# State-space branch: masked products, steps, one subtraction and the chunk recurrence as wide GpSimd calls, with fewer VectorE instructions

## The chip, the cores and the metric

The kernel runs on one core of a Trainium2 chip. That core has five engines that run side by side, each with its own in-order queue of instructions: TensorE (PE, with its weight loads shown apart as PEld), VectorE (DVE), ScalarE (ACT), GpSimd (POOL) and SyncE (SP, which here only starts transfers). They wait for one another through semaphores. The metric is the device time of one execution in microseconds (us), lower is better.

## The reference, cut to what matters

Two transformer-like blocks work on one sequence of 512 tokens of 1024 features. The first block has an attention branch and a state-space branch in parallel, then cross attention and a feed-forward part; the second has a gated delta rule, sparse attention and a mixture of experts. Only the state-space branch of the first block is touched. It has 32 heads in 8 groups of 4; the heads of a group share B and C. The sequence is cut into 4 chunks of 128 tokens, and every head runs in two directions, forward and backward. In plain notation, for one chunk and one head, with cs the running sum of the step sizes times a decay rate:

```
S   = B . C^T                                       (128 x 128, shared by the 4 heads)
E   = exp(min(cs_f[l] - cs_f[s], cs_b[l] - cs_b[s]))   forward and backward decay in one
M   = E * S * (dt_f[s] where l >= s, plus dt_b[s] where l <= s)
y   = M^T . x + dskip * x                            inside the chunk
h_f[c+1] = raw_f[c] + tot_f * h_f[c]                 states handed on, chunk by chunk
h_b[c-1] = raw_b[c] + tot_b * h_b[c]
y  += C . h_f * exp(cs_f) + C . h_b * exp(cs_b)      then gate, norm, projection
```

## The kernel before, in words

All matrix products of weights are done as three products of split operands (a high and a low part of each), so every weight that comes in is first split: ACT casts the high part (line 269), DVE subtracts to get the low part (line 272). Then PE runs the three products, `mm3`, lines 277 to 279, in tiles named `mm`.

The branch goes group by group. `ssd_in` projects B, C, x and z of a group and runs a short convolution over them (four DVE instructions per tile, line 638). `ssd_p1` does the part inside the chunks: transposes of x and B (`xt`, `bt`), the products B.C^T (`cb` on PE, copied by ACT to the tile `CB`), and then for each of the four chunks: weighted inputs `xw` (POOL), step tiles `D` (POOL: two masked products and their sum), the chunk's states `st` (PE, copied by ACT into `pv`), the two tiles `cs` that a DMA broadcasts from DRAM, their difference and minimum, the exponential, the products with `CB` and `D`, a skip term `sk` (POOL), and the products `yd` (PE). `ssd_p2` hands the states on from chunk to chunk, multiplies them with C (`yo`), gates the result and sums its squares; `ssd_p3` normalizes and transposes (`yt`).

The difference and the minimum are done head by head before the change, two instructions for each head:

```
for h in range(4):
    nc.scalar.activation(cb[0][:, h, :], cb[0][:, h, :], AF.Identity, bias=...)
    nc.vector.scalar_tensor_tensor(cb[0][:, h, :], cb[1][:, h, :], self.cs[...], cb[0][:, h, :],
                                   op0=OP.subtract, op1=OP.min)
```

What sets the order: the program is written in the order above, but a scheduler lays out each engine's queue ahead of time from its own costs and from the priorities of the program order. So projections of the group after next stand between the chunk's steps on PE, as cover for the time that the other engines need for a chunk. Once laid out, every queue is fixed: an instruction that waits holds up all that stand behind it on its engine. Tiles of the pool `g` come from a ring of 25 buffers; a new tile waits until the buffer's last reader is done.

Of the kernel before, what the change touches and what calls it, by code (L numbers as in the profile page):

```python
# [38 lines left out]
def host_arrays(inp):  # L39
# [128 lines left out]
class Emit:  # L168
# [30 lines left out]
    def psum(self, stack, n, mm, sa, sm):  # L199
        """the eight banks: dense products, two kinds of chains"""  # L200
# [30 lines left out]
    # ---------------------------------------------------------------- tools  # L231
# [49 lines left out]
    def proj_b(self, ps, units, act, halves=False):  # L281
        """feature-major: ps[128 cols, n tok]; units: list of W along K; act(k) -> (hi, lo)
        halves: the first half of the tokens as soon as it is there"""
# [19 lines left out]
    def proj_a(self, banks, units, act):  # L303
        """token-major: banks: psum tiles, two token tiles of 256 columns each; act(k, t) -> (hi, lo)"""
# [11 lines left out]
    def split(self, hi, lo, src, scale=None):  # L316
        """hi + lo = src * scale (scale: per-partition AP or None)"""
# [11 lines left out]
    def rstd(self, out, ss, n, eps=EPS):  # L329
        """out = (ss / n + eps) ** -0.5"""  # L330
# [5 lines left out]
    def rsqrt(self, v, eps, scale=1.0, tile=None):  # L336
        """(scale * v + eps) ** -0.5: a first guess from the bits, then Newton's iteration"""
# [13 lines left out]
    def norm_out(self):  # L351
        """where normed rows go, transposed and split: put(t, h, x) takes half a tile; hT(k) -> (hi, lo)"""
# [14 lines left out]
    def norm_T(self, gname):  # L367
        """rmsnorm of token-major tiles, transposed and split: step(t, x) takes a tile"""
# [80 lines left out]
    def attn_in(self):  # L449
        nc, a = self.nc, self.a  # L450
        # keys: natural and half-swapped, split
# [19 lines left out]
    def attention(self):  # L471
        nc, a = self.nc, self.a
        # the result of a tile of queries takes the place of the queries
# [77 lines left out]
    def dt_section(self):  # L551
# [44 lines left out]
        self.dtdec = self.dec  # L596
        self.ncs = self.cp.tile([128, 4, 32], F32, name="ncs")
# [4 lines left out]
    def gates1(self, f0, f1):  # L602
        """tanh of the halved gates, feature-major, to DRAM"""
# [10 lines left out]
    def branch_a(self):  # L614
        """(1 + tanh(ga / 2)) * (attn @ Wa), feature-major, to DRAM"""
# [11 lines left out]
    def conv(self, ps, ct, ntap, first, silu_scale=True):  # L627
        """half of the centred depthwise convolution of a psum tile, then 2 * half * sigmoid = silu"""
# [15 lines left out]
    def ssd_in(self, g):  # L644
        """projections of group g: B, C, x (feature-major, convolved) and the doubled silu of z (token-major)"""
# [18 lines left out]
    def ssd_p1(self, g, inp):  # L664
        """the part inside the chunks, and the chunks' states"""
# [4 lines left out]
        # token-major x and B  # L670
# [19 lines left out]
        # D[s, l]: the step of the forward direction for l >= s and that of the backward one for l <= s  # L690
        D = []

        def steps(c):
            d = [self.G("D", (128, 4, 128)) for _ in range(2)]
            for i, m in enumerate((self.MU, self.ML)):
                nc.gpsimd.tensor_tensor(d[i], m[:, None, :].to_broadcast([128, 4, 128]),
                                        self.dt[:, c, i, H][:, :, None].to_broadcast([128, 4, 128]), op=OP.mult)
            nc.gpsimd.tensor_tensor(d[0], d[0], d[1], op=OP.add)
            D.append(d[0])

        # per chunk: the part inside the chunk, and the chunk's states
        pv = [self.G("pv", (128, 2, 256)) for _ in range(4)]
# [4 lines left out]
        for c in range(4):  # L707
# [4 lines left out]
            steps(c)  # L712
# [6 lines left out]
            # raw states into the slot that they feed: forward c + 1, backward c - 1  # L719
            if c < 3:  # L720
                nc.scalar.copy(pv[c + 1][:, 0, :], ps[:, 0:256])
            if c > 0:
                nc.scalar.copy(pv[c - 1][:, 1, :], ps[:, 256:512])
            cb = []
            for d in range(2):
# [3 lines left out]
                cb.append(t)  # L729
            for h in range(4):  # L730
# [1581 lines left out]
```

## Time and profile before

| | |
|---|---|
| runs of the kernel before | 2174.90, 2181.30, 2185.06 us; median 2181.3 us |
| span of the profiled execution, first to last instruction | 2182.1 us |
| PE busy | 2033.9 us (93%) |
| DVE busy | 1362.7 us (62%) |
| ACT busy | 892.3 us (41%) |
| POOL busy | 504.9 us (23%), 515 instructions |
| mean granted TensorE clock | 0.961 |

How to read it: the profile records one execution. Its span is the only time that the profile has of that execution; it lies 0.8 us from the median of the runs. PE is busy for most of the span, so what counts is where PE stands still and what it waits for there, and in which stretches its clock was granted below full speed (0.5 in a row of clocks is 1.2 GHz, 1.0 is 2.4 GHz). The state-space branch is the stretch from about 300 to 850 us.

### The profile page before, as it was taken

The numbers are of one execution on the slowest core, as the hardware profiler recorded it, in microseconds if no ns is written. First come the engines' busy times: TensorE is split into PE (matmuls) and PEld (weight loads), VectorE is DVE, ScalarE is ACT, GpSimd is POOL, SyncE is SP. The second block draws the span as 40 slices with busy tenths as digits, with TensorE's granted clock in tenths as the row PEclk, the third lists the DMA queues.
The fourth block names the chain that finished last, engine by engine and source line by source line (L and its number), as shares of the span: only waits on it lengthen the run. The fifth ranks groups of instructions, "written<-read, shape, count | busy, mean of one in ns | idle before, by whom it ended". The sixth has DMA issues, their size and how long they took to land. (4 is left out here: it accounts for less than half of the span.)

```text
span 2182.1 us, 31237 instructions
## 1 busy us (share of the span) xinstructions
PE 2033.9 (93%) x11818; PEld 1730.2 (79%) x11818; DVE 1362.7 (62%) x2622; ACT 892.3 (41%) x1630; POOL 504.9 (23%) x515
## 2 busy tenths in 40 slices
PE   7999988989999988999999999899899999998995
PEld 7788877877787777888999999787878768886774
DVE  4566446786978765466334444667789452538885
ACT  4344434444545343254323222542232333246773
POOL 0000034034433142101111101503511110224444
PEclk9999999999999999999999999998899899998997
DMA  4211234323333254422222223224212104677976
GB/s 168 84 67 63 78 101 159 116 72 112 94 107 100 88 157 157 156 88 69 97 97 96 88 97 116 97 79 122 91 50 76 45 21 158 223 296 245 324 269 165
DMA packets 131302, 266.71 MB, mean 122 GB/s; under 512 B 22256, under 2 KB 67696, under 8 KB 127050
## 3 DMA queue, kind: packets, MB, share of 16 engines
q1 hardware_dynamic: 127690, 256.26, 35.5%
q0 software_dynamic: 3456, 8.39, 1.7%
q8 instruction: 95, 1.56, 0.3%
q14 instruction: 61, 0.50, 0.1%
HBM read 242.93 MB, written 25.35 MB: 123 GB/s over the span
## 5 line engine op out<-in xcount | busy, mean ns | idle before, releaser
L272 DVE TENSOR_TENSOR wl<-wr,wh 128x1024 fp32r<-128x1024 f32 (+1 forms) x272 | 316.4, 1164 | 288.9 <-ACT wh L269 277.9
L269 ACT CAST wh<-wr 128x1024 fp32r<-128x1024 f32 (+1 forms) x272 | 264.5, 973 | 548.5 <-PE mm L278 282.8
L279 PE MATMUL mm<-hTh,wl 128*128 128x512 f32 (+1 forms) x1056 | 412.4, 391 | 1.3 <-DVE wl L272 1.3
L277 PE MATMUL mm<-hTh,wh 128*128 128x512 f32 (+1 forms) x1056 | 411.9, 390 | 1.6 <-ACT hTh L320 0.9
L278 PE MATMUL mm<-hTl,wh 128*128 128x512 f32 (+1 forms) x1056 | 410.7, 389 | 0.8 <-DVE hTl L321 0.8
L279 PEld LDWEIGHTS mm<-hTh,wl 128*128 128x128 f32 x1056 | 203.4, 193 | 42.4 <-issue 5.1
L277 PEld LDWEIGHTS mm<-hTh,wh 128*128 128x128 f32 x1056 | 203.2, 193 | 39.6 <-issue 2.6
L278 PEld LDWEIGHTS mm<-hTl,wh 128*128 128x128 f32 x1056 | 203.2, 192 | 39.2 <-issue 3.2
L710 POOL TENSOR_TENSOR xw<-xt,dtT 128x256 f32<-128x256 f32 (+1 forms) x32 | 29.8, 932 | 551.4 <-ACT xt L678 551.4
L278 PE MATMUL mm<-wl,hTh 128*128 128x256 f32 x512 | 150.1, 293 | 0.0
L277 PE MATMUL mm<-wh,hTh 128*128 128x256 f32 x512 | 149.8, 293 | 0.0
L279 PE MATMUL mm<-wh,hTl 128*128 128x256 f32 x512 | 149.3, 292 | 0.0
L278 PE MATMUL mm<-wl,uh 128*128 128x256 f32 x512 | 145.0, 283 | 0.0
L279 PE MATMUL mm<-wh,ul 128*128 128x256 f32 x512 | 144.8, 283 | 0.0
L277 PE MATMUL mm<-wh,uh 128*128 128x256 f32 x512 | 144.7, 283 | 0.0
L876 DVE SCALAR_TENSOR_TENSOR x<-mm,x 128x256 f32<-128x256 f32 x152 | 57.5, 420 | 93.4 <-PE mm L279 92.8
L1042 POOL TENSOR_TENSOR ul<-r,uh 128x512 fp32r<-128x512 f32 x32 | 41.7, 1303 | 274.8 <-ACT uh L1041 274.8
L278 PEld LDWEIGHTS mm<-wl,hTh 128*128 128x128 f32 x512 | 100.9, 197 | 1.7 <-issue 0.7
L277 PEld LDWEIGHTS mm<-wh,hTh 128*128 128x128 f32 x512 | 100.8, 197 | 1.0 <-issue 0.2
L279 PEld LDWEIGHTS mm<-wh,hTl 128*128 128x128 f32 x512 | 100.8, 197 | 0.7 <-issue 0.5
L278 PEld LDWEIGHTS mm<-wl,uh 128*128 128x128 f32 x512 | 98.2, 192 | 0.5 <-DVE wl L272 0.2
L277 PEld LDWEIGHTS mm<-wh,uh 128*128 128x128 f32 x512 | 98.2, 192 | 0.3
(571 smaller groups left out, 4706.2 us busy)
## 6 DMA issues: line engine op xcount, KB each, us to landing
mr<-in_w_egu_dram SPq DMA_DIRECT2D x32, 1024.0 KB, 8.4
wr<-in_win_b_dram SPq DMA_DIRECT2D x59, 512.0 KB, 3.3
cs<-csd SPq DMA_DIRECT2D x64, 256.0 KB, 4.5
wr<-in_w_up_dram SPq DMA_DIRECT2D x32, 512.0 KB, 3.3
wr<-in_w_down_dram SPq DMA_DIRECT2D x32, 512.0 KB, 3.3
wr<-in_w_ed_dram SPq DMA_DIRECT2D x32, 512.0 KB, 4.5
wr<-in_w_b_dram SPq DMA_DIRECT2D x29, 512.0 KB, 3.3
wr<-in_win_a_dram SPq DMA_DIRECT2D x18, 512.0 KB, 3.3
```

The costliest lines, as they stand in the source:

```text
L269: nc.scalar.copy(w.hi, raw)
L272: e.tensor_tensor(w.lo, raw, w.hi.bitcast(F32), op=OP.subtract)
L277: mm(out, lh, rh, start=start, stop=False, skip_group_check=skip)
L278: mm(out, lh, rl, start=False, stop=False, skip_group_check=skip)
L279: mm(out, ll, rh, start=False, stop=stop, skip_group_check=skip)
L710: nc.gpsimd.tensor_tensor(xw[:, d0:d1], h3(xt[c])[:, None].to_broadcast([128, d1 - d0, 4, 64]), self.dtdec[:, c, d0:d1, H][:, :, :, None]. ...
L876: nc.vector.scalar_tensor_tensor(xv, ps[t // 2][:, (t % 2) * 256:(t % 2 + 1) * 256], scale, xv, op0=OP.mult, op1=OP.add)
L1042: nc.gpsimd.tensor_tensor(ul[:, j, :], r, uh[:, j, :].bitcast(F32), op=OP.subtract)
```

## The change

Five things are rewritten. The masks now multiply `CB` instead of the steps: two tiles `CBt` for each group, made on POOL. `D` is made from `CBt`, so it already holds B.C^T, and DVE's product with `CB` is gone. The backward subtraction of the four heads is one POOL instruction on the whole tile; DVE is left with one minimum for all heads. The recurrence over chunks pairs both directions in one slot (`pv[k]` holds the forward state of chunk k and the backward state of chunk 3 - k), and takes two POOL products and two POOL sums for a group in place of sixteen DVE instructions. The factors for that are copied once into a tile `stp`. `yo` products of the two middle chunks are two products of 256 columns each, since the directions now lie in different slots. Comments and texts of functions are removed as well, which moves line numbers.

```diff
+        self.stp = self.cp.tile([128, 2, 2, 32], F32, name="stp")
+        for k in range(2):
+            nc.gpsimd.tensor_copy(self.stp[:, k, 0], self.tot[:, k + 1, 0])
+            nc.gpsimd.tensor_copy(self.stp[:, k, 1], self.tot[:, 2 - k, 1])
...
         nc.scalar.copy(CB, ps.rearrange("p (c l) -> p c l", c=4))
-        D = []
+        CBt = [self.G("CBt", (128, 4, 128)) for _ in range(2)]
+        for i, m in enumerate((self.MU, self.ML)):
+            nc.gpsimd.tensor_tensor(CBt[i], CB, m[:, None, :].to_broadcast([128, 4, 128]), op=OP.mult)
 
         def steps(c):
             d = [self.G("D", (128, 4, 128)) for _ in range(2)]
-            for i, m in enumerate((self.MU, self.ML)):
-                nc.gpsimd.tensor_tensor(d[i], m[:, None, :].to_broadcast([128, 4, 128]),
+            for i in range(2):
+                nc.gpsimd.tensor_tensor(d[i], CBt[i][:, c, None, :].to_broadcast([128, 4, 128]),
                                         self.dt[:, c, i, H][:, :, None].to_broadcast([128, 4, 128]), op=OP.mult)
             nc.gpsimd.tensor_tensor(d[0], d[0], d[1], op=OP.add)
-            D.append(d[0])
+            return d[0]
...
-                nc.scalar.copy(pv[c + 1][:, 0, :], ps[:, 0:256])
+                nc.scalar.copy(pv[c][:, 0, :], ps[:, 0:256])
...
-                nc.scalar.copy(pv[c - 1][:, 1, :], ps[:, 256:512])
+                nc.scalar.copy(pv[3 - c][:, 1, :], ps[:, 256:512])
...
+            nc.gpsimd.tensor_tensor(cb[1], cb[1], self.cs[:, c, 1, H][:, :, None].to_broadcast([128, 4, 128]), op=OP.subtract)
             for h in range(4):
                 nc.scalar.activation(cb[0][:, h, :], cb[0][:, h, :], AF.Identity, bias=self.ncs[:, c, 4 * g + h:4 * g + h + 1])
-                nc.vector.scalar_tensor_tensor(cb[0][:, h, :], cb[1][:, h, :], self.cs[:, c, 1, 4 * g + h:4 * g + h + 1],
-                                               cb[0][:, h, :], op0=OP.subtract, op1=OP.min)
+            nc.vector.tensor_tensor(cb[0], cb[0], cb[1], op=OP.min)
             nc.scalar.activation(cb[0], cb[0], AF.Exp)
-            nc.vector.tensor_tensor(cb[0], cb[0], CB[:, c, None, :].to_broadcast([128, 4, 128]), op=OP.mult)
-            nc.vector.tensor_tensor(cb[0], cb[0], D[c], op=OP.mult)
+            nc.vector.tensor_tensor(cb[0], cb[0], D, op=OP.mult)
...
-        for d, order in ((0, (2, 3)), (1, (1, 0))):
-            for c in order:
-                p = c - 1 if d == 0 else c + 1
-                for h in range(4):
-                    hs = slice(64 * h, 64 * h + 64)
-                    nc.vector.scalar_tensor_tensor(pv[c][:, d, hs], pv[p][:, d, hs], self.tot[:, p, d, 4 * g + h:4 * g + h + 1],
-                                                   pv[c][:, d, hs], op0=OP.mult, op1=OP.add)
+        for k in range(2):
+            q = self.G("pq", (128, 2, 256))
+            nc.gpsimd.tensor_tensor(v(q), v(pv[k]), self.stp[:, k, :, H][:, :, :, None].to_broadcast([128, 2, 4, 64]), op=OP.mult)
+            nc.gpsimd.tensor_tensor(pv[k + 1], pv[k + 1], q, op=OP.add)
```

How the queues stand. First POOL's queue at the start of a group's `ssd_p1` (the second group; the others are alike), before the change:

```order
L710 TENSOR_TENSOR xw<-xt,dtT 128x256
L696 TENSOR_TENSOR D<-consts,dtT 128x512 x2
L698 TENSOR_TENSOR D<-D 128x512
L738 TENSOR_TENSOR sk<-xt,vecs 128x256
L333 TENSOR_SCALAR ssq<-ssq 128x4
L334 TENSOR_TENSOR rsy<-ssq,mhalf 128x4
L710 TENSOR_TENSOR xw<-xt,dtT 128x512
L696 TENSOR_TENSOR D<-consts,dtT 128x512 x2
```

and in the same place after it:

```order
L698 TENSOR_TENSOR CBt<-CB,consts 128x512 x2
L719 TENSOR_TENSOR xw<-xt,dtT 128x256
L704 TENSOR_TENSOR D<-CBt,dtT 128x512 x2
L706 TENSOR_TENSOR D<-D 128x512
L746 TENSOR_TENSOR sk<-xt,vecs 128x256
L333 TENSOR_SCALAR ssq<-ssq 128x4
L334 TENSOR_TENSOR rsy<-ssq,mhalf 128x4
L739 TENSOR_TENSOR cs<-cs,dtT 128x512
L719 TENSOR_TENSOR xw<-xt,dtT 128x512
```

The two `CBt` products, which need the copy of `CB`, now stand ahead of the first `xw`, and the first chunk's subtraction (`cs<-cs,dtT`) stands behind its `D`, its `sk` and the two small steps of the norm of the group before (`ssq`, `rsy`).

Second, POOL's queue further on in the same group, after the change, from the third chunk's sum of steps on:

```order
L706 TENSOR_TENSOR D<-D 128x512
L746 TENSOR_TENSOR sk<-xt,vecs 128x256
L739 TENSOR_TENSOR cs<-cs,dtT 128x512 x2
L719 TENSOR_TENSOR xw<-xt,dtT 128x256
L704 TENSOR_TENSOR D<-CBt,dtT 128x512 x2
L706 TENSOR_TENSOR D<-D 128x512
L746 TENSOR_TENSOR sk<-xt,vecs 128x256
L766 TENSOR_TENSOR pq<-pv,stp 128x512
L767 TENSOR_TENSOR pv<-pv,pq 128x512
L766 TENSOR_TENSOR pq<-pv,stp 128x512
L767 TENSOR_TENSOR pv<-pv,pq 128x512
L739 TENSOR_TENSOR cs<-cs,dtT 128x512
```

The subtractions of the second and the third chunk stand together, behind the steps and the skip term of the third; that of the fourth stands behind the whole recurrence.

Third, PE's queue in the last group, around the `yd` of the second and the third chunk, after the change:

```order
L749 MATMUL yd<-xt,cs 128x64 x4
L726 MATMUL st<-xw,Bt 128x256 x2
L278 MATMUL mm<-hTl,wh 128x512
L279 MATMUL mm<-hTh,wl 128x512
L277 MATMUL mm<-hTh,wh 128x512
L278 MATMUL mm<-hTl,wh 128x512
L279 MATMUL mm<-hTh,wl 128x512
L749 MATMUL yd<-xt,cs 128x64 x4
```

Five products of 512 columns stand between `st` and `yd` of the third chunk there (3 to 10 in the other groups); in the same place before the change there are 29 in the last group, and 32 to 40 in the first two.

## Rows read from the trace of the kernel before

**Rows 1.** Busy time of each engine in the stretch of the state-space branch.

```profile
core 0: us, PE busy (x) PEld busy (x) DVE busy (x) ACT busy (x) POOL busy (x), PEclk, DMA share, GB/s
300.00:850.00 550.00, 498.71 (x2573) 418.87 (x2572) 415.99 (x841) 248.06 (x526) 193.94 (x182) 0.95 0.37 111
```

**Rows 2.** Waits of PE from 300 to 850 us: total us, times, longest.

```profile
PE yd L741 <- DVE cs L736: 42.2, 17, 5.7
```

**Rows 3.** Timeline of PE, seventh group: start, duration, operation, idle before.

```profile
695.87 0.59 PE L717 MATMUL st<-xw,Bt 128*128 128x256 f32 x2
...
704.80 1.08 PE L741 MATMUL yd<-xt,cs 128*128 128x64 f32 x8 [0.16 <-DVE cs L736]
...
706.46 1.03 PE L717 MATMUL st<-xw,Bt 128*128 128x256 f32 x4
...
716.19 0.39 PE L278 MATMUL mm<-hTl,wh 128*128 128x512 f32 x1
716.42 0.39 PE L279 MATMUL mm<-hTh,wl 128*128 128x512 f32 x1
721.88 1.97 PE L741 MATMUL yd<-xt,cs 128*128 128x64 f32 x8 [5.08 <-DVE cs L736]
723.64 2.02 PE L717 MATMUL st<-xw,Bt 128*128 128x256 f32 x4
```

**Rows 4.** The same view: first and last of PE's 17 waits for that product.

```profile
316.56 1.94 PE L741 MATMUL yd<-xt,cs 128*128 128x64 f32 x8 [5.66 <-DVE cs L736]
...
816.80 1.10 PE L741 MATMUL yd<-xt,cs 128*128 128x64 f32 x8 [1.74 <-DVE cs L736]
```

**Rows 5.** Timeline of POOL, seventh group, from its first to its third chunk.

```profile
694.27 0.61 POOL L710 TENSOR_TENSOR xw<-xt,dtT 128x256 f32<-128x256 f32 x1 [28.14 <-ACT xt L678]
694.84 2.22 POOL L696 TENSOR_TENSOR D<-consts,dtT 128x512 f32<-128x512 f32 x2
697.14 1.35 POOL L698 TENSOR_TENSOR D<-D 128x512 f32<-128x512 f32 x1
...
700.35 0.19 POOL L333 TENSOR_SCALAR ssq<-ssq 128x4 f32<-128x4 f32 x1 [1.10 <-ACT sq L776]
...
701.62 1.04 POOL L710 TENSOR_TENSOR xw<-xt,dtT 128x512 f32<-128x512 f32 x1
...
713.25 0.61 POOL L738 TENSOR_TENSOR sk<-xt,vecs 128x256 f32<-128x256 f32 x1
```

**Rows 6.** Timeline of DVE, seventh group, ahead of the wait of 5.08 us.

```profile
708.50 1.53 DVE L641 SCALAR_TENSOR_TENSOR cv<-ct,cv 128x512 f32<-128x512 f32 x1
...
715.10 3.13 DVE L732 SCALAR_TENSOR_TENSOR cs<-cs,dtT 128x128 f32<-128x128 f32 x4
...
721.15 0.68 DVE L736 TENSOR_TENSOR cs<-cs,D 128x512 f32<-128x512 f32 x1
```

**Rows 7.** Timeline of ACT, seventh group: copy of B.C^T, and one exponential.

```profile
695.63 0.59 ACT L689 COPY CB<-cb 128x512 f32<-128x512 f32 x1 [0.46 <-PE cb L687]
...
718.27 0.63 ACT L734 ACTIVATE cs<-cs 128x512 f32<-128x512 f32 x1 [6.03 <-DVE cs L732]
```

**Rows 8.** POOL instructions by line: count, duration min/median/max in ns.

```profile
L696 POOL TENSOR_TENSOR D<-consts,dtT x64: 1034/1042/2041, 300.2 to 788.4; 128x512 f32<-128x512 f32 x64
L698 POOL TENSOR_TENSOR D<-D x32: 1261/1350/2160, 303.3 to 789.6; 128x512 f32<-128x512 f32 x32
L1534 POOL TENSOR_TENSOR E<-E,consts x8: 1262/1278/1549, 1501.3 to 1535.9; 128x512 f32<-128x512 f32 x8
```

**Rows 9.** DVE instructions by line, in the same form.

```profile
L732 DVE SCALAR_TENSOR_TENSOR cs<-cs,dtT x128: 336/347/1457, 307.6 to 812.3; 128x128 f32<-128x128 f32 x128
L735 DVE TENSOR_TENSOR cs<-cs,CB x32: 677/692/1522, 313.2 to 815.3; 128x512 f32<-128x512 f32 x32
L759 DVE SCALAR_TENSOR_TENSOR pv<-pv,dtT x128: 271/280/1321, 323.5 to 807.8; 128x64 f32<-128x64 f32 x128
```

**Rows 10.** Issues of DMA on the page: count, KB each, us to landing.

```profile
cs<-csd SPq DMA_DIRECT2D x64, 256.0 KB, 4.5
```

More of the change, by code (lines that the diff above doesn't have):

```diff
@@ L689, in ssd_p1 @@
         nc.scalar.copy(CB, ps.rearrange("p (c l) -> p c l", c=4))
-        D = []
+        CBt = [self.G("CBt", (128, 4, 128)) for _ in range(2)]
+        for i, m in enumerate((self.MU, self.ML)):
+            nc.gpsimd.tensor_tensor(CBt[i], CB, m[:, None, :].to_broadcast([128, 4, 128]), op=OP.mult)
         def steps(c):
             d = [self.G("D", (128, 4, 128)) for _ in range(2)]
-            for i, m in enumerate((self.MU, self.ML)):
-                nc.gpsimd.tensor_tensor(d[i], m[:, None, :].to_broadcast([128, 4, 128]),
+            for i in range(2):
+                nc.gpsimd.tensor_tensor(d[i], CBt[i][:, c, None, :].to_broadcast([128, 4, 128]),
                                         self.dt[:, c, i, H][:, :, None].to_broadcast([128, 4, 128]), op=OP.mult)
             nc.gpsimd.tensor_tensor(d[0], d[0], d[1], op=OP.add)
-            D.append(d[0])
-        pv = [self.G("pv", (128, 2, 256)) for _ in range(4)]
+            return d[0]
+        pv = [self.G("pv", (128, 2, 256)) for _ in range(3)]
         h3 = lambda ap: ap.rearrange("p (h d) -> p h d", h=4)
@@ L711, in ssd_p1 @@
                                     self.dtdec[:, c, d0:d1, H][:, :, :, None].to_broadcast([128, d1 - d0, 4, 64]), op=OP.mult)
-            steps(c)
+            D = steps(c)
             ps = self.PA("st")
@@ L753, in ssd_p2 @@
         yc = lambda c: ys[c // 2][:, (c % 2) * 256:(c % 2 + 1) * 256]
-        for d, order in ((0, (2, 3)), (1, (1, 0))):
-            for c in order:
-                p = c - 1 if d == 0 else c + 1
-                for h in range(4):
-                    hs = slice(64 * h, 64 * h + 64)
-                    nc.vector.scalar_tensor_tensor(pv[c][:, d, hs], pv[p][:, d, hs], self.tot[:, p, d, 4 * g + h:4 * g + h + 1],
-                                                   pv[c][:, d, hs], op0=OP.mult, op1=OP.add)
+        v = lambda t: t.rearrange("p d (h e) -> p d h e", h=4)
+        for k in range(2):
+            q = self.G("pq", (128, 2, 256))
+            nc.gpsimd.tensor_tensor(v(q), v(pv[k]), self.stp[:, k, :, H][:, :, :, None].to_broadcast([128, 2, 4, 64]), op=OP.mult)
+            nc.gpsimd.tensor_tensor(pv[k + 1], pv[k + 1], q, op=OP.add)
         ssq = self.S("ssq", 4)
@@ L765, in ssd_p2 @@
             d0, d1 = (1 if c == 0 else 0), (1 if c == 3 else 2)
-            nc.tensor.matmul(po[:, 256 * d0:256 * d1], CT[:, ts[c]], pv[c][:, d0:d1, :].rearrange("p a b -> p (a b)"),
-                             start=True, stop=True)
+            for d in range(d0, d1):
+                nc.tensor.matmul(po[:, 256 * d:256 * d + 256], CT[:, ts[c]], pv[2 - c if d else c - 1][:, d, :], start=True, stop=True)
             y = yc(c)
```

## The prediction

> **What bounds the kernel now.** I read the busy times by stretch first. In the 550 us of the state-space branch PE is busy for 498.7, so it stands still for 51.3 us, and its clock was granted at 0.95 of full speed [rows 1]. The list of PE's waits says where: 42.2 us in 17 pieces in front of `yd`, for DVE's last product on the `cs` tile [rows 2]; about 9 us are left for everything else. So the branch is PE-bound with a hole at `yd`, and a change there is worth at most those 42 us, plus what the holes do to the clock.
>
> The timelines of one group show how a hole arises. PE reaches `yd` of the second chunk after 716.42 + 0.23 and waits 5.08 us [rows 3]. On DVE the last links of that chain stand late in a full queue: four subtract-and-minimum instructions take 3.13 us, though one alone has a median of 347 ns, and the last product ends at 721.83 [rows 6, 9]. POOL is running its `D` products in this stretch; a DVE or POOL instruction that meets the other's is stretched, DVE's to 1457 ns at most, POOL's `D` from 1042 to 2041 [rows 8, 9]. After the wait, `yd` and `st` take 1.97 and 2.02 us, against 1.08 and 1.03 one chunk earlier: half clock, the 1.2 GHz level [rows 3]. The same shows after nine of the 17 waits, all six over 3 us and three of the 11 shorter ones; the first and the last are examples of either [rows 4]. I count at least 1.9 us for such a phase from these two instructions, and take 2.5.
>
> **What it takes off DVE.** For each chunk four subtract-and-minimum instructions (4 x 0.347) become one minimum of 512 columns, which the trace does not show; the nearest row is the product with `CB`, 0.69. That product itself goes (0.69). For each group sixteen recurrence instructions (16 x 0.280) go [rows 9]. At medians that is 5.55 - 2.77 + 2.77 + 4.48 = 10.0 us a group, 80 us in all. This is no gain by itself: it counts only where DVE was last in the chain, as in [rows 6].
>
> **What it puts on POOL.** Two `CBt` products read two full streams; the nearest row is the mask product of line 1534, 1.28 each. Four subtractions have one operand that is constant along the inner axis, as L696 has: 1.04 each, with L698's 1.35 as the other end. Two recurrence products at 1.04 and two sums at 1.35 [rows 8]. That is 2.6 + 4.2 + 4.8 = 11.6 us a group, 93 us in all. POOL has the room on average (194 of 550 us [rows 1]); but all of it lies in the short stretch of `ssd_p1`, in one queue, and every subtraction is now a link of the chain to `yd`.
>
> **The sum along POOL's queue, from the end of B.C^T on PE to `yd` of the second chunk.** ACT's copy of `CB`: 0.59 and a hand-over, 0.7 [rows 7]. Then POOL in the order that the queue shows: two `CBt` 2.6; the first chunk's `xw`, `D`, `D`, sum, `sk` 0.57 + 2.1 + 1.3 + 0.6 = 4.6; the norm's two small steps 1.3; the subtraction 1.0; two further chunks with a wide `xw` at 5.0 each; the second subtraction 1.0: 20.5 us [rows 5, 8]. What the meeting with DVE adds: before, the stretch from 694.27 to 713.86 holds 15.9 us of the same work and 1.1 us of idling, so 2.6 were lost [rows 5]. With fewer two-operand DVE instructions I take 2.0, with 0 and 4 as bounds. Then minimum 0.69, exponential 0.63, product 0.69 and three hand-overs of 0.05: 2.2 [rows 6, 7, 9]. Sum 25.4 us.
>
> PE's cover for that: in the new order 67 to 83 products of 512 columns stand between B.C^T and this `yd`, 76 on average, at 0.23 each, and `st`, `st`, `yd` at 0.3, 0.7 and 0.9: 19.4 us [rows 3]. So PE loses **6.0 us** by then: about 2 in front of the first `st` (its `xw` now stands behind both `CBt`, 0.7 + 2.6 + 0.6 against 7 to 9 products), the rest at the two `yd`. Bounds 4.0 and 8.0.
>
> The third chunk costs nothing: its subtraction follows the second's directly. In the fourth, the subtraction stands behind the recurrence, which needs the last `st`: 0.3, a copy of the states (half as wide as that of `CB`, estimated 0.4), 4.8, 1.0, and 2.2 again, 8.7 us. Its cover is 22 to 26 products of 512 columns, or about 58 of 256 at half of 0.23: 6.3 us on average. **2.4 us** more; with DVE in the way up to 3.5.
>
> Together 8.4 us a group, 67 in all, in place of 42.2: **+25**, between +9 (no meeting with DVE) and +50. Per group that makes four short holes. At three in 11 for the short ones, and two or three of the eight second chunks over 3 us, I expect about 12 half-clock phases in place of 9: **+8**, between 0 and +20. Of the 9 us of other waits the lighter DVE may take **-4**, between 0 and -9. 2182.1 + 25 + 8 - 4 = 2211 us against the profiled span; the median of the runs lies 0.8 lower, so **2210 us**.
>
> **Costed at nothing.** The sixteen further `yo` products stream the same columns; at most 0.23 each, 4 us. The four copies to `stp` lie in POOL's idle time ahead of a group, 28 us here [rows 5]. The ring of 25 buffers now serves three more tiles a group; the worst that I would expect is one POOL instruction of 1.04 a group, 8 us. The DMAs for `cs` of the second and third chunk stand behind a weight load whose buffer comes free only after DVE's first last-link product and the split behind it: about 13 us after B.C^T, then 1.2, two issues, and 4.5 to land [rows 10], 20 us, while POOL asks for them at 22. That cover is 2 us; without it every further microsecond is lost at `yd`. Behind the minimum, DVE's queue holds convolution steps and the next weights' low part; PE needs them only after the same `yd`.
>
> **A rule weighed.** By [rows 8, 9] a product of 512 columns takes 1.04 to 1.35 us on POOL and 0.69 on DVE, and what is moved here is moved onto the chain. The Trainium skill (GPSIMD Engine Reference, 4.1 Engine selection) advises VectorE for elementwise work on tiles and puts GpSimd at about half its speed with two inputs. By that rule the 93 us are the price of 80, and the rows agree.
>
> **Rivals.**
> - *The two engines take full turns.* In [rows 6] a DVE instruction of 0.69 takes 1.53 us beside POOL's `xw`. If every second of POOL's 21 instructions up to the second subtraction waits out one DVE instruction of 0.69, that is 7 us in place of 2, and 3 more behind it: 17 us a group, 136 in all, +94 and +15 by the clock: 2291 us. Against it: POOL lost only 2.6 us in a stretch in which DVE was full. The Trainium skill (SBUF — State Buffer, Who interferes with whom) has exactly this: a DVE instruction with two SBUF inputs and a GpSimd instruction that reads SBUF lock each other out for a whole instruction. Single pairs in the trace agree, the loss over the stretch does not. Chance 0.10.
> - *Nothing to measure.* No loss between the engines, 51 us of waits in place of 42, no further clock phases, all other waits gone: 2182 + 9 - 9 = 2182, or a little around it. Chance 0.17.
> - *Faster: DVE was the limit, and POOL is not.* DVE's backlog made the 5.08 us, and 10 us a group of it go. If POOL is never last, half of the 42 us and half of the nine clock phases vanish: -21 - 11, 2150 us. It decides from the point where POOL ends the second subtraction 19.4 - 0.7 - 2.2 = 16.5 us after the copy of `CB`; its queue holds 20.5 at unstretched durations, so PE would have to come 4 us later for other reasons. Chance 0.15.
>
> **Chances and range.** The forecast, POOL's queue longer than PE's cover, holds 0.58, and its own range is 2193 to 2245. Faster or slower than before can be told from no change by about 0.5%, 11 us. Faster 0.15; same 0.18, the second rival and an edge of the forecast; slower 0.67. From 2170 to 2248 the forecast and the second rival are in, most of the first and the third rival out.
>
> **What would show it.** PE's list: `st` with a wait for POOL's `xw` of about 2 us a group, eight times, which is absent now; `yd` still waiting for DVE, 4 to 8 us a group in all, and DVE's minimum waiting for POOL's subtraction as the longest DVE wait. POOL busy about 93 us more, close to unbroken from `CBt` to the last subtraction. DVE some 80 to 110 us less. I am wrong if the minimum finds its subtraction done, or if PE comes to `yd` later than the order's count of products says.

## The result, and the profile after

The changed kernel takes 2205.6 us (median of 4 runs, 2201.2 to 2208.0) against 2182.3 (2174.9 to 2185.1) on the same chip: 1.011 times the time before, 95% interval 1.0086 to 1.0133, so slower by 0.9 to 1.3%. The forecast was 2210, range 2170 to 2248.

The page, busy time by engine (us, share of the span, instructions):

```profile
PE 2030.5 (92%) x11850; PEld 1732.5 (79%) x11850; DVE 1299.9 (59%) x2366; ACT 892.5 (40%) x1630; POOL 617.4 (28%) x599
```

POOL has 112.5 us more than before, DVE 62.8 less; PE's sum is the same to 4 us. So over the whole program PE works as long as before: the time is in its waits. The stretch of the branch (columns as in [rows 1]), and PE's waits from 290 to 900 us (total, times, longest), which answer to [rows 2]:

```profile
300.00:850.00 550.00, 480.14 (x2442) 408.74 (x2440) 330.55 (x540) 233.74 (x495) 296.35 (x257) 0.93 0.34 105
```

```profile
PE yd L749 <- DVE cs L744: 47.2, 23, 3.7
PE st L726 <- POOL xw L719: 19.4, 8, 3.0
```

66.6 us in 31 pieces stand where 42.2 in 17 stood. They are shorter (3.7 at most, 5.7 before) and more. By chunk, added up over the eight groups from PE's timeline (small waits that the list leaves out included):

| PE waits, us | `st` | `yd` 1st chunk | 2nd | 3rd | 4th | sum |
|---|---|---|---|---|---|---|
| before | 0 | 13.1 | 25.1 | 2.3 | 1.8 | 42.2 |
| after | 19.4 | 12.1 | 13.7 | 3.5 | 17.9 | 66.6 |

So the change did shorten the wait of the second chunk, by 11 us; it pays 19 at `st` and 16 at the fourth `yd`. Up to the second `yd` the sum grows by 7 us only (38.2 to 45.2); 16 of the 24 us come at the fourth. The seventh group on PE's timeline (start, duration, operation, idle before), beside [rows 3]:

```profile
722.99 1.05 PE L692 MATMUL cb<-cv 128*128 128x128 f32 x8
...
728.24 0.70 PE L726 MATMUL st<-xw,Bt 128*128 128x256 f32 x2 [2.14 <-POOL xw L719]
...
739.25 1.10 PE L749 MATMUL yd<-xt,cs 128*128 128x64 f32 x8 [1.90 <-DVE cs L744]
...
750.94 1.15 PE L749 MATMUL yd<-xt,cs 128*128 128x64 f32 x8 [1.67 <-DVE cs L744]
...
756.29 1.00 PE L749 MATMUL yd<-xt,cs 128*128 128x64 f32 x8
...
768.89 1.96 PE L749 MATMUL yd<-xt,cs 128*128 128x64 f32 x8 [2.81 <-DVE cs L744]
```

and POOL's timeline in the same group, beside [rows 5]:

```profile
724.75 2.69 POOL L698 TENSOR_TENSOR CBt<-CB,consts 128x512 f32<-128x512 f32 x2 [17.65 <-ACT CB L694]
727.40 0.79 POOL L719 TENSOR_TENSOR xw<-xt,dtT 128x256 f32<-128x256 f32 x1
...
733.37 1.84 POOL L739 TENSOR_TENSOR cs<-cs,dtT 128x512 f32<-128x512 f32 x1
...
746.65 1.06 POOL L746 TENSOR_TENSOR sk<-xt,vecs 128x256 f32<-128x256 f32 x1
747.68 1.04 POOL L739 TENSOR_TENSOR cs<-cs,dtT 128x512 f32<-128x512 f32 x1
```

POOL runs without a gap from 724.75 to the end of the second subtraction at 748.72, 24.0 us; `yd` of that chunk starts at 750.94, 2.2 behind it. From the end of `cb` (724.04) that is 26.9 us, of which PE waited 2.14 + 1.90 + 1.67 = 5.7: its cover is 21.2. The prediction had 25.4, 19.4 and 6.0. ("Cover" is here PE's time from the end of B.C^T to a `yd` without its idle time.)

### The profile page after: what moved, and what is told of

It reads as the page before. It is cut to its first block, busy times and chain, and to the rows that moved or that the text cites. A ratio compares the mean times of both kernels' runs of the same rounds, so it can differ in the third digit from the quotient of the medians.

```text
span 2206.2 us, 31052 instructions
## 1 busy us (share of the span) xinstructions
PE 2030.5 (92%) x11850; PEld 1732.5 (79%) x11850; DVE 1299.9 (59%) x2366; ACT 892.5 (40%) x1630; POOL 617.4 (28%) x599
## 5 line engine op out<-in xcount | busy, mean ns | idle before, releaser
L272 DVE TENSOR_TENSOR wl<-wr,wh 128x1024 fp32r<-128x1024 f32 (+1 forms) x272 | 324.5, 1193 | 305.2 <-ACT wh L269 296.3
L698 POOL TENSOR_TENSOR CBt<-CB,consts 128x512 f32<-128x512 f32 x16 | 24.2, 1536 | 442.6 <-ACT CB L694 442.6
L643 DVE SCALAR_TENSOR_TENSOR cv<-mm,vecs,cv 128x510 f32<-128x510 f32 (+1 forms) x128 | 95.3, 745 | 13.8 <-ACT cv L636 12.1
```

Of the source, the lines that this page charges most:

```text
L272: e.tensor_tensor(w.lo, raw, w.hi.bitcast(F32), op=OP.subtract)
L643: nc.vector.scalar_tensor_tensor(ov, iv, self.cw(ct, tap), ov, op0=OP.mult, op1=OP.add)
L698: nc.gpsimd.tensor_tensor(CBt[i], CB, m[:, None, :].to_broadcast([128, 4, 128]), op=OP.mult)
```

## The experiments

One table holds all of them. "Ratio" is the time over that of the kernel before on the same chip, with its interval. The other columns are from the trace of each profiled execution: "stage" from the first `cb` to the end of the last `yd`, "waits" PE's idle time in it (at `yd` and at `st` apart), "work" the rest, "512" the number of products of 512 columns in it, and "1.2 GHz" the time in it, in us, for which the record of the granted clock has the lower level.

| kernel | ratio | stage | waits | at `yd` | at `st` | work | 512 | 1.2 GHz |
|---|---|---|---|---|---|---|---|---|
| before | 1 | 517.8 | 45.0 | 42.2 | 0 | 472.8 | 1247 | 51 |
| after | 1.0110 (1.0086 to 1.0133) | 545.3 | 69.6 | 47.2 | 19.4 | 475.7 | 1202 | 72 |
| e1 `xw` first | 1.0234 (1.0200 to 1.0268) | 557.6 | 77.3 | 69.3 | 0 | 480.3 | 1204 | 96 |
| e2 subtraction ahead of recurrence | 1.0124 (1.0093 to 1.0156) | 538.7 | 65.8 | 42.5 | 19.2 | 472.9 | 1202 | 68 |
| e3 one more POOL product | 1.0251 (1.0221 to 1.0280) | 554.4 | 74.7 | 45.8 | 25.6 | 479.7 | 1217 | 75 |
| e4 subtraction on ACT | 0.9992 (0.9966 to 1.0019) | 507.8 | 44.7 | 15.9 | 21.8 | 463.1 | 1230 | 31 |
| e5 subtraction on DVE | 1.0184 (1.0151 to 1.0217) | 544.5 | 66.8 | 38.6 | 19.2 | 477.7 | 1215 | 72 |
| e6 C.B product on DVE | 1.0167 (1.0142 to 1.0193) | 549.0 | 66.6 | 63.2 | 0 | 482.4 | 1214 | 89 |
| e7 recurrence on DVE | 1.0055 (1.0033 to 1.0077) | 524.4 | 56.6 | 34.8 | 20.2 | 467.8 | 1202 | 55 |
| e8 recurrence alone on POOL | 1.0073 (1.0045 to 1.0101) | 525.3 | 53.8 | 50.1 | 0 | 471.5 | 1220 | 61 |
| e9 PE's order of before | 1.0114 (1.0083 to 1.0145) | 540.1 | 62.5 | 32.4 | 21.2 | 477.6 | 1202 | 75 |
| e10 e4 with `xw` first | 0.9905 (0.9874 to 0.9937) | 492.4 | 36.3 | 29.5 | 0 | 456.1 | 1229 | 20 |
| e11 subtraction alone, on ACT | 0.9871 (0.9833 to 0.9908) | 488.4 | 32.0 | 24.6 | 0 | 456.4 | 1233 | 17 |
| e12 subtraction alone, on POOL | 1.0033 (1.0008 to 1.0057) | 518.7 | 51.5 | 49.0 | 0 | 467.2 | 1214 | 58 |

The stages explain most of the ratios, not all. Behind the branch the same program, and up to 45 products of 512 columns (10 us) that a stage leaves to it, takes 1351 to 1383 us in these profiles (1364 before, 1361 after), with no wait of the branch in it. What differs there most is the granted clock: from 1355 to 1605 us it is 0.92 in e3, and from 1345 to 1595 us 0.96 in the changed kernel. Differences between two kernels of less than about 10 us are therefore not read here.

**e1: is the wait at `st` a loss by itself?** The first chunk's `xw` goes ahead of the two `CBt`.

```diff
+        xw0 = weigh(0)
         CBt = [self.G("CBt", (128, 4, 128)) for _ in range(2)]
...
-            xw = self.G("xw", (128, 2, 4, 64))
+            xw = weigh(c) if c else xw0
```

> The first chunk's xw is issued ahead of the two CBt products; nothing else is changed. Theory A (POOL's queue from B.C^T to the second subtraction is longer than PE's cover): the queue is as long as before, so the 19.4 us of waits at the first st vanish and come back at the yd of the second chunk, whose waits grow by 15 to 20 us; PE's cover is 1 or 2 products of 512 columns (0.23 us each) shorter in most groups. Time 2206, within 2198 to 2214. Rival B (each wait is a loss by itself): st costs nothing any more and yd stays at 47, time 2187.

PE's waits in the stretch:

```profile
PE yd L755 <- DVE cs L750: 69.3, 26, 5.9
```

and POOL's for the transfers of `cs`:

```profile
POOL cs L745 <- DMA cs<-csd: 22.9, 14, 3.5
```

The `st` row is gone and `yd` has 22.1 us more, as Theory A had it: 19.4 us moved, none was won. They moved to the first `yd` (12.1 to 36.2), whose subtraction stands in the same queue. Seven of its eight waits are now 4.2 to 6.0 us, and after each of the seven `yd` takes 1.9 to 2.0 us, the 1.2 GHz level. At the second chunk POOL now waits for the transfer in seven of the eight groups, 0.6 to 2.8 us; in the changed kernel it did so in one. Rival B falls. The time is above the range (2230 for 2206). Of the 21 us between the two profiled executions 12.3 are in the stage, 7.7 of them waits; 9.1 lie behind the branch, which the queue does not explain. In the stage the lower clock was granted for 96 us in place of 72.

**e2: is the fourth chunk late because its subtraction stands behind the recurrence?**

```diff
+        with self.tc.issue_after(self.last.ins):       # the fourth subtraction
             for k in range(2):
                 q = self.G("pq", (128, 2, 256))
```

> The recurrence's four POOL instructions are queued behind the fourth chunk's subtraction instead of ahead of it; the work is the same. Theory A: the waits at the yd of the fourth chunk (2.5 to 3.7 us in six groups, 17.9 us in all) go, and what follows them at half clock, some 4 us; the recurrence comes 1 us later and yo has cover. Time 2186, within 2179 to 2196. Rival B (the fourth chunk is late because DVE or ACT is, not because POOL is): the subtraction is done early and the wait stays, time 2206.

2207.6 us: no gain, and waits at the fourth `yd` of 15.6 us in place of 17.9. This part of the theory falls, but not for the rival's reason. POOL's timeline (seventh group):

```profile
755.07 1.60 POOL L746 TENSOR_TENSOR sk<-xt,vecs 128x256 f32<-128x256 f32 x1
762.24 1.04 POOL L739 TENSOR_TENSOR cs<-cs,dtT 128x512 f32<-128x512 f32 x1 [5.57 <-DMA cs<-csd]
763.24 1.05 POOL L767 TENSOR_TENSOR pq<-pv,stp 128x512 f32<-128x512 f32 x1
764.36 1.60 POOL L768 TENSOR_TENSOR pv<-pv,pq 128x512 f32<-128x512 f32 x1
```

and those of DVE and SP:

```profile
763.31 1.51 DVE L742 TENSOR_TENSOR cs<-cs 128x512 f32<-128x512 f32 x1 [2.33 <-POOL cs L739]
...
766.07 0.67 DVE L744 TENSOR_TENSOR cs<-cs,D 128x512 f32<-128x512 f32 x1
```

```profile
756.26 0.34 SPq L266 DMA_DIRECT2D wr<-in_w_sb_dram  x1
756.70 0.94 SPq L737 DMA_DIRECT2D cs<-csd  x2
```

The subtraction, free of the recurrence, stands 5.57 us for its transfer, which SP issues from 756.70 on right behind a weight load; these transfers take 4.8 us to land (median). Such loads wait for DVE, by the waits of SP from 740 to 765 us:

```profile
SPq L266 <- DVE wl L272: 24.7, 3, 12.8
```

And the minimum, now beside the recurrence, takes 1.51 us for 0.69. Counted from the second subtraction of the group (747.15 in e2, 747.68 in the changed kernel), the fourth came 2.4 us earlier (15.1 us behind it for 17.5), the product behind it 1.6.

**e3: does one more POOL product cost its own length?**

```diff
+        cx = self.G("cx", (128, 4, 128))
+        nc.gpsimd.tensor_tensor(cx, CB, self.MU[:, None, :].to_broadcast([128, 4, 128]), op=OP.mult)
```

> One more POOL product per group, 128x512, behind the two CBt (its result is used by nobody). Theory A: POOL's queue ahead of the second subtraction is the limit, so every group is later by 1.3 to 1.5 us, 11 us in all, plus up to 6 for further phases at half clock: 2218, within 2211 to 2228; waits at st and yd together 77 us in place of 67. Rival B (POOL has slack and DVE or the cs transfers end last): 2206.

2233.6 us, above the range. Its waits are 71.4 us at `st` and `yd` (66.6 in the changed kernel; 77 expected), and the stage is 9.1 us longer: 5.1 of waits and 4.0 of work, with 15 more products of 512 columns in it. The stretch from B.C^T to the second `yd` takes 29.3 us in place of 27.0. So POOL has no slack, and Rival B falls. The profiled executions differ by 17.5 us; 7.7 of them lie behind the branch, where the clock differed, and are not explained by the queue, and neither is what the medians (28 us apart) have beyond that.

**e4: the subtraction taken off POOL, onto ACT.** Everything else stays as changed.

```diff
-            nc.gpsimd.tensor_tensor(cb[1], cb[1], self.cs[:, c, 1, H][:, :, None].to_broadcast([128, 4, 128]), op=OP.subtract)
-            for h in range(4):
-                nc.scalar.activation(cb[0][:, h, :], cb[0][:, h, :], AF.Identity, bias=self.ncs[:, c, 4 * g + h:4 * g + h + 1])
+            for d, n in enumerate((self.ncs, self.ncb)):
+                for h in range(4):
+                    nc.scalar.activation(cb[d][:, h, :], cb[d][:, h, :], AF.Identity, bias=n[:, c, 4 * g + h:4 * g + h + 1])
             nc.vector.tensor_tensor(cb[0], cb[0], cb[1], op=OP.min)
```

> The subtraction goes to ACT, as four biased copies per chunk of 128x128, as the forward half already does; masks, steps, C.B and recurrence stay on POOL, the minimum stays one wide DVE instruction. Theory A: POOL's queue up to the second chunk's D is about 14 us against 19 of cover, and the fourth chunk no longer stands behind the recurrence; the waits at yd fall from 47 to 10 us or less, those at st (19) stay, the clock gives back about 8: 2163, within 2150 to 2180. Rival B (it is DVE's meetings with POOL, not POOL's queue, that make yd late): 30 us or more of waits stay at yd, 2190 to 2200. Rival C (ACT's 128 more instructions at some 0.3 us, 38 us, become the last link): yd waits for the minimum and the minimum for ACT, 2195 or more.

```profile
PE st L728 <- POOL xw L721: 21.8, 8, 3.0
PE yd L751 <- DVE cs L746: 15.9, 16, 3.0
```

The waits at `yd` fall from 47.2 to 15.9 us (10 or less were expected) with DVE's load unchanged (1295.1 us busy for 1299.9) and POOL's other work unchanged. The time at 1.2 GHz falls from 72 to 31 us and the work of the stage by 12.6. Rivals B and C fall; 2175.2 us is inside the range. That it was the subtraction's place in POOL's queue does not follow: the order on PE changed too (see the table under e10 to e12).

**e5 to e8: the parts undone one by one, and the recurrence alone.**

```diff
@@ e5 (and e8) @@
-            nc.vector.tensor_tensor(cb[0], cb[0], cb[1], op=OP.min)
+                nc.vector.scalar_tensor_tensor(cb[0][:, h, :], cb[1][:, h, :], self.cs[:, c, 1, 4 * g + h:4 * g + h + 1],
+                                               cb[0][:, h, :], op0=OP.subtract, op1=OP.min)
@@ e6 (and e8) @@
-                nc.gpsimd.tensor_tensor(d[i], CBt[i][:, c, None, :].to_broadcast([128, 4, 128]),
+                nc.gpsimd.tensor_tensor(d[i], m[:, None, :].to_broadcast([128, 4, 128]),
+            nc.vector.tensor_tensor(cb[0], cb[0], CB[:, c, None, :].to_broadcast([128, 4, 128]), op=OP.mult)
@@ e7 @@
-            nc.gpsimd.tensor_tensor(v(q), v(pv[k]), ...)
-            nc.gpsimd.tensor_tensor(pv[k + 1], pv[k + 1], q, op=OP.add)
+                    nc.vector.scalar_tensor_tensor(pv[k + 1][:, d, hs], pv[k][:, d, hs], ..., op0=OP.mult, op1=OP.add)
```

> Of the changed kernel only the subtraction is undone: DVE takes four subtract-and-minimum instructions per chunk again; CBt, D and the recurrence stay on POOL. Theory A: POOL is never last at yd (its queue up to the second D is about 14 us against 19 of cover), the fourth chunk isn't behind the recurrence; yd waits for DVE alone, whose load is 58 us below that of the kernel before (22 of the C.B product, 36 of the recurrence), so 10 to 25 us at yd in place of 47, and 19 at st as now: 2178, within 2165 to 2190. Rival B (DVE's length is the limit): DVE is longer than in the changed kernel by 22 us, 2206 or more.

> Of the changed kernel only the masks are undone: POOL multiplies masks and steps, DVE takes the product with C.B again; subtraction and recurrence stay on POOL. Theory A: the queue no longer begins with the copy of C.B and two CBt (0.7 + 2.6 us): st waits for nothing (-19), the second subtraction is about 17.9 us behind B.C^T against 19 of cover, the fourth chunk keeps about half of its wait since its cover is 32 to 36 products in place of 26 to 29. DVE has 22 us more. Waits at yd 15 to 30: 2172, within 2160 to 2190. Rival B (any subtraction on POOL costs what the whole change costs): yd stays at 47, 2187 or more.

> Of the changed kernel only the recurrence is undone: sixteen small DVE instructions a group again; CBt, D and the subtractions stay on POOL. Theory A: st 19 and the second yd as in the changed kernel, the fourth chunk's 18 us go since nothing long stands ahead of its subtraction; DVE has some 36 us more, which may cost a few: 2190, within 2182 to 2204. Rival B (taking the recurrence off DVE is what keeps the changed kernel from being worse): 2215 or more.

> Of the change only the recurrence on POOL is kept; masks, subtraction and the product with C.B are those of the kernel before. Theory A: POOL's queue is that of the kernel before up to the fourth D, the recurrence lies behind it with cover at yo; DVE loses 36 us: the 42 us at yd fall to 25 to 40, 2172, within 2160 to 2184. Rival B (the order that the new dependencies give PE, with the third chunk's yd only 4 to 12 products behind its st in place of 32 to 42, is what costs): the waits at yd grow to 50 or more, 2190 and above.

Only e7 came as expected (2188 us). e5 (2219), e6 (2215) and e8 (2193) are all slower than Theory A gave, and in each it is Rival B's number that came. Three different reasons were named for it; that of e5, DVE's length, does not hold, since e11 below has more work on DVE (1347.0 us for 1339.1) and is 74 us faster. What the three have in common is the recurrence on POOL. Beside its partner without it, each version with it has more waits at the fourth `yd`: 17.9 for 5.6 (after and e7), 17.5 for 1.6 (e6 and e12, below), 10.7 for 1.8 (e8 and before). In e8 no subtraction is on POOL, so it can't be the place of the subtraction. DVE's timeline of e8, seventh group:

```profile
741.76 0.74 DVE L643 SCALAR_TENSOR_TENSOR cv<-mm,vecs,cv 128x510 f32<-128x510 f32 x1
...
743.55 1.53 DVE L646 SCALAR_TENSOR_TENSOR cv<-ct,cv 128x512 f32<-128x512 f32 x1
745.01 1.52 DVE L643 SCALAR_TENSOR_TENSOR cv<-mm,vecs,cv 128x510 f32<-128x510 f32 x2
746.45 2.96 DVE L738 SCALAR_TENSOR_TENSOR cs<-cs,dtT 128x128 f32<-128x128 f32 x4
749.33 0.74 DVE L643 SCALAR_TENSOR_TENSOR cv<-mm,vecs,cv 128x511 f32<-128x511 f32 x1
749.99 0.68 DVE L272 TENSOR_TENSOR wl<-wr,wh 128x512 fp32r<-128x512 f32 x1
750.59 0.68 DVE L741 TENSOR_TENSOR cs<-cs,CB 128x512 f32<-128x512 f32 x1
```

and POOL's:

```profile
742.76 1.78 POOL L764 TENSOR_TENSOR pq<-pv,stp 128x512 f32<-128x512 f32 x1 [9.49 <-ACT pv L729]
744.62 1.63 POOL L765 TENSOR_TENSOR pv<-pv,pq 128x512 f32<-128x512 f32 x1
746.32 1.04 POOL L764 TENSOR_TENSOR pq<-pv,stp 128x512 f32<-128x512 f32 x1
747.44 1.29 POOL L765 TENSOR_TENSOR pv<-pv,pq 128x512 f32<-128x512 f32 x1
```

From 742.76 to 748.73 POOL runs the recurrence. In these six us DVE's instructions with two SBUF operands take twice their time: 1.53 for 0.68, and 2.96 for four that take 0.34 each where POOL stands still. Those with one operand in PSUM (`mm`) keep theirs, 0.74 each. What is stretched is the fourth chunk's chain, which always meets the recurrence, since that starts from the fourth chunk's states. Over the branch the 128 subtract-and-minimum instructions average 635 ns in e8 and 475 before. The Trainium skill (SBUF — State Buffer, Who interferes with whom) states that a DVE instruction with two SBUF inputs and a GpSimd instruction that reads SBUF exclude each other; these rows agree. In e8 PE also has less to do ahead of the fourth `yd` than before (37.7 us for 44.0), so its waits there are not the stretched chain alone.

**e9: is it the order on PE?** Every version above lets PE come to the third `yd` 2 to 15 products of 512 columns behind the third `st` (two of 256 counted as one), where it was 29 to 42 before.

```diff
+                for c, k in ((2, 152), (3, 190)) if g else ():
+                    self.tc.add_manual_dep(self.ydm[c].ins, self.rec[k].ins.name, ...)   # yd behind this product
```

> The changed kernel with PE's queue as in the kernel before at two places: in the third to the seventh group the yd of the third chunk comes behind 8 to 23 products of 512 columns and 55 to 57 of 256, that of the fourth behind 30 to 33 of 256 and some more; all else is the changed kernel's. Theory C (formed on e2 and e8: every version of the change lets PE come to the third and fourth yd some 20 to 30 products of 512 columns sooner than the kernel before, and that, not only POOL's work, leaves the chain of the fourth chunk uncovered): the waits there, 14.2 us at the fourth and 2.8 at the third yd in these groups, go, and some 4 us of half clock with them; st and the first two yd stay: 2186, within 2178 to 2196. Rival A (the chain is that much longer than before that the cover doesn't matter, or the buffers that are held longer delay the next group): 2200 or more.

```profile
PE yd L754 <- DVE cs L749: 32.4, 15, 3.7
PE st L731 <- POOL xw L724: 21.2, 8, 3.2
...
PE yo L781 <- DVE yl L329: 3.1, 2, 1.5
PE yo L781 <- POOL pv L774: 2.6, 1, 2.6
```

In the five groups the third and fourth `yd` lose 10 of the expected 17 us (7.2 are left at the fourth); the first `yd` loses 4 more. Of these 5 are left in the stage: `yo`, `st` and the weight splits wait more in exchange, and the chain of the fourth chunk comes later along with PE (the table under e10 to e12). 2202.7 us; Theory C is at most a fifth of the loss.

**e10 to e12: what the parts are worth once the subtraction is off POOL.** e10 is e4 with the edit of e1. e11 and e12 are the kernel before with the wide minimum and the subtraction on ACT (the edit of e4) or on POOL (as changed); C.B and recurrence as before.

> The version with the subtraction on ACT, and the first chunk's xw ahead of the CBt products. Theory A: with the subtraction off POOL there is slack ahead of the first two yd (they wait 0 to 3 us in that version), so the 21.8 us of waits at the first st go and only some 6 to 10 us come back at yd, unlike in the version with the subtraction on POOL, where all of them came back: 2161, within 2150 to 2172. Rival B (the wait only moves, as it did there): 2175.

> The kernel before with one thing changed: the backward half of the subtraction on ACT as four biased copies, the minimum one wide DVE instruction; masks, product with C.B and recurrence as before, on POOL, DVE and DVE. If taking DVE's load is what helps (theory D), this version, with 22 us of C.B products and 36 us of recurrence more on DVE than the version with all three moved and the subtraction on ACT, is slower than that one by 10 us or more, 2172 or above against 2161 for it with xw first. If only the links of the chain to yd count (theory A), it has none on POOL, no wait at st, and the minimum in one piece: 2162, within 2150 to 2172.

> The kernel before with one thing changed: the subtraction is one wide POOL instruction, the minimum one wide DVE instruction; masks, product with C.B and recurrence as before. Its DVE work is that of the version with the subtraction alone on ACT (2145), so the two differ by the engine of the subtraction alone. Theory A (the subtraction's place in POOL's queue, behind the steps of the third chunk, is what makes the second yd late): no waits at st, the first and second yd wait together some 4 to 6 us a group, the fourth less than in the version that has the recurrence on POOL too (63 us at yd, 2215); 45 us at yd and several phases at half clock: 2192, within 2180 to 2205. Rival D (the relief of DVE by the wide minimum is what the version on ACT lives on, wherever the subtraction is done): 2150, within 2143 to 2165.

2156.6, 2145.3 and 2183.0 us, the first inside its range, the second 5 us below it, the third inside. In e10 the waits at `st` (21.8 us) go and 13.6 come back at `yd`. e11 is the fastest kernel of the study, 1.3% below the one before, with 47 us more on DVE than the changed kernel: Theory D falls. e11 and e12 run the same DVE instructions, have the subtraction on different engines and differ by 1.6%. PE's waits in the two, e11 first:

```profile
PE yd L749 <- DVE cs L744: 22.2, 15, 3.3
...
PE yd L749 <- ACT cs L740: 2.5, 2, 1.4
```

```profile
PE yd L747 <- DVE cs L742: 49.0, 17, 5.6
```

In e12 `yd` of the second chunk waits 4.7 to 5.6 us in five groups, 1.1 to 2.2 in the same groups of e11. The seventh group, from the last `cb` products on PE, e11 with ACT's timeline first:

```profile
676.51 0.38 PE L694 MATMUL cb<-cv 128*128 128x128 f32 x2
...
695.70 1.28 ACT L740 ACTIVATE cs<-cs,ncs 128x128 f32<-128x128 f32 x4 [2.03 <-DMA cs<-csd]
696.94 1.28 ACT L740 ACTIVATE cs<-cs,ncb 128x128 f32<-128x128 f32 x4
```

and e12 with POOL's:

```profile
705.01 0.38 PE L692 MATMUL cb<-cv 128*128 128x128 f32 x2
...
723.59 0.61 POOL L744 TENSOR_TENSOR sk<-xt,vecs 128x256 f32<-128x256 f32 x1
724.20 3.12 POOL L736 TENSOR_TENSOR cs<-cs,dtT 128x512 f32<-128x512 f32 x2
```

From the end of B.C^T the second chunk's subtraction starts after 20.1 us on ACT, which had waited for the transfer, and after 18.8 us on POOL, behind the third chunk's steps. So its place in POOL's queue did not make it later. All groups, in us from the end of B.C^T, means of eight; "512" is the number of products of 512 columns ahead of the second `yd`:

| kernel | 2nd subtraction starts | 2nd chunk's last product ends | PE's cover to 2nd `yd` | 512 | 4th `yd` starts | PE's cover to 4th `yd` |
|---|---|---|---|---|---|---|
| before | - | 26.5 | 21.6 | 79 | 49.6 | 44.0 |
| after | 23.3 | 27.0 | 21.4 | 76 | 44.2 | 35.5 |
| e3 | 25.0 | 29.3 | 23.0 | 79 | 46.0 | 36.6 |
| e4 (ACT) | 22.8 | 27.4 | 23.3 | 85 | 44.1 | 38.5 |
| e6 | 19.5 | 27.2 | 22.2 | 79 | 45.9 | 37.5 |
| e9 | 23.6 | 27.2 | 21.8 | 74 | 48.8 | 41.0 |
| e11 (ACT) | 20.5 | 26.5 | 23.5 | 87 | 43.7 | 39.7 |
| e12 | 19.4 | 27.1 | 21.5 | 79 | 43.7 | 37.2 |

With the subtraction on ACT the stretches up to the two `yd` are as long as with it on POOL (27.4 for 27.0 and 44.1 for 44.2 in e4 and the changed kernel, 43.7 both times in e11 and e12). What grew is PE's cover, by 2 to 3 us a group: the scheduler laid out PE's queue anew and put some nine more products of 512 columns ahead of the second `yd`. Behind the subtraction the chain is 1.7 us shorter in e11 (6.0 us for 7.7), but it starts 1.1 later. So the gain of e4 and e11 goes with PE's order at least as much as with the engine. No run moves the subtraction and keeps PE's order, so the two are not separated; that more products ahead of a `yd` don't pay by themselves, e9 shows.

## Why the prediction was right, and where it was not

**POOL's queue against PE's cover: right, by e1 and e3.** 6.0 us a group were forecast up to the second `yd`, about 2 of them at `st`. It is 45.2 us over eight groups, 5.6 each, 2.4 at `st`. e1 shows that these are one debt and not three waits, e3 that a longer queue makes it larger. Some luck is in the size: in the seventh group the queue took 26.9 us for 25.4 and PE's cover was 21.2 for 19.4: two errors of nearly 2 us that cancel. PE coming later than the count says was one of the two named signs of being wrong. That the subtraction in this queue makes the debt is not shown: taken off POOL, it starts 0.5 us earlier (e4 for the changed kernel) or 1.1 later (e11 for e12). And POOL's queue is not alone at the end of it. The transfers for the second chunk were costed at nothing with 2 us to spare. SP issues them, together with those of the third, behind a weight load (seventh group):

```profile
741.43 0.35 SPq L266 DMA_DIRECT2D wr<-in_w_sb_dram  x1
741.87 2.04 SPq L737 DMA_DIRECT2D cs<-csd  x4
```

That is 17.8 us after B.C^T, where 13 + 1.2 were taken. The one that POOL needs goes 0.5 us later and takes 4.8 to land, 23.1 us (an estimate from these rows); POOL asks at 23.6. Half a microsecond is left, and e1 used it up.

**The fourth chunk: right in size, wrong in cause.** This is the larger part of the slowdown, 16 of 24 us. 2.4 us a group were forecast for a subtraction that stands behind the recurrence; 17.9 / 8 = 2.2 came. But e2 took the recurrence out of its way and won nothing. Two other things were seen to hold that chain: its transfer, issued behind a weight load that waits for DVE's split, in e2 lands 5.6 us after POOL could use it; and whatever of the chain meets the recurrence on DVE takes twice as long. The first was costed at nothing for the second and third chunk, with a cover of 2 us; the sum never asked for the fourth. The second is the pairwise turn-taking that the first rival had over the whole stretch: over the stretch it did not come (2291 us), for the fourth chunk it did. Which of the two is the larger was not separated; the transfer on another queue was not run. A third is PE's order, with 35.5 us of cover where it was 44.0; e9 gave back 5.5 of them, and the fourth `yd` came 4.6 us later. So the cause of the fourth chunk's wait stays open beyond this: with the recurrence on POOL it is there (three pairs above), and in e6 against e12 at equal cover (37.5 and 37.2 us) the fourth `yd` comes 2.2 us later.

**DVE's relief: 63 us for 80, POOL's load: 112.5 for 93.** The durations were medians of undisturbed rows. By line, from 290 to 880 us (count, busy, mean ns, idle before and what ended it):

```profile
L742 DVE TENSOR_TENSOR cs<-cs 128x512 f32<-128x512 f32 x32 | 32.9, 1027 | 64.3 <-POOL cs L739 59.7 <-ACT cs L741 3.6 <-issue 1.0
```

```profile
L739 POOL TENSOR_TENSOR cs<-cs,dtT 128x512 f32<-128x512 f32 x32 | 38.0, 1190 | 8.8 <-DMA cs<-csd 8.8
...
L698 POOL TENSOR_TENSOR CBt<-CB,consts 128x512 f32<-128x512 f32 x16 | 24.2, 1536 | 442.6 <-ACT CB L694 442.6
L767 POOL TENSOR_TENSOR pv<-pv,pq 128x512 f32<-128x512 f32 x16 | 23.6, 1473 | 1.3
```

The minimum averages 1027 ns where 692 was taken, `CBt` 1536 for 1280, the recurrence's sums 1473 for 1350: together the meetings took 11 us of the relief on the minimum alone. The idle time in the first row is the sign that was named: the minimum waits 59.7 us for POOL's subtraction, DVE's longest wait. The 8.8 us in the second are the transfers that were costed at nothing.

**The clock: +8 forecast, about +13 by an estimate.** The stage has 16 stretches at 1.2 GHz for 9 before (12 were forecast), 72 us for 51. PE was busy in 70.3 of them for 44.9; at half pace that is 12.7 us more. The work of the stage shows only 2.9 of it (475.7 us for 472.8), since 45 products of 512 columns (10 us) are no longer in it. **Other waits: -4 forecast, 0 measured** (2.8 us of the stage's idle time are elsewhere before, 3.0 after). The waits at `st` and `yd` are 66.6 us for 67. **The rest of the program: nothing forecast.** It does those 45 products as well and is still 3.5 us shorter, with a granted clock of 0.975 for 0.957. It is not read as the change's: whole executions of the kernel before were granted 0.959 to 0.973. So 24.1 us between the profiled executions, for 29 forecast, are a good sum of the waits and some luck.

**The weighed rule** (the Trainium skill, GPSIMD Engine Reference, 4.1 Engine selection: about half of VectorE's speed with two inputs) is borne out by 112 us paid for 63. The Trainium skill, Perfetto Trace Analysis (Optimizing Scalar/DVE Operations), holds that moving work between GpSimd and DVE may not help, and that ScalarE may take some where DVE is saturated; the first agrees with the changed kernel, and e11 gained 1.3% with DVE busy for 63% of the span.

**The parts.** The recurrence on POOL costs 0.6 to 1.3% in three pairs (after and e7, before and e8, e12 and e6). The masks and the product with C.B have no sign of their own: without the recurrence they make no difference (e7 against e12, 0.2%), beside it they read as 1.1% slower (e5 against e8) and 0.6% faster (after against e6). The faster rival did not come: the minimum waited 59.7 us for POOL. Without DVE's narrow subtract-and-minimum instructions e11 is 33 us faster than the kernel before, but PE's order differs between the two as well (87 and 79 products ahead of the second `yd`).

## What to carry to other kernels

Before work is moved to an engine that is idle on average, write down its queue in the stretch where the moved result is needed: an instruction costs what stands ahead of it, not its own length. A wait that vanishes by reordering one queue can turn up whole at the next reader of that queue (here 19.4 us gone at `st`, 22.1 more at `yd`). Where a link of a chain must move, try also an engine that does not slow the next link while it works; here ACT took it for 1.28 us a chunk, and the kernel gained 1.3%. And before such a gain is put down to the moved instruction, count what each queue does ahead of the wait in both versions: here the link came no earlier, but the bottleneck engine's queue had been laid out anew.

## What was not expected of the hardware

A POOL stretch of six us doubled the DVE instructions inside it that read two SBUF operands (1.53 us for 0.68) and left those that read PSUM as they were (0.74), while POOL's own took up to 1.78 for 1.04: POOL's load on DVE's chain is a matter of the moment, not of the average. And the time at 1.2 GHz went with the waits: 51 us of the stage with 42.2 us at `st` and `yd` before, 72 with 66.6 after, 17 with 24.6 in e11. One run has nearly the same waits in longer pieces: e1, 69.3 us with pieces up to 5.9, where 1.2 GHz was granted for 96 us.
